# When the gate's sum is split and multiplied, in a hybrid convolution and RG-LRU layer

## The chip, the cores and the metric

The kernel runs on one core of a Trainium2 chip, in one launch. The metric is the time of one execution on the device in microseconds (us), taken as the median of several runs. A profiled execution also leaves a trace, which records when each instruction ran on each engine: PE (TensorE, matrix products), PEld (its weight loads), DVE (VectorE), ACT (ScalarE), POOL (GpSimd) and SP (the queue that issues the DMAs).

## The reference, cut to what matters

One layer on 512 latent tokens and 256 context tokens of width 2048. The input projection has six column groups; the gate `gt_l`, which the change is about, scales the output projection.

```python
mod_lat = silu(c) @ w_ada + b_ada
sh_l, sc_l, gt_l = split(mod_lat, 3)
...
hl = rmsnorm(x, norm_g) * (1 + sc_l) + sh_l
b, c, u, g, v, q = split(hl @ w_in)
ya = b * conv3(c * u) * silu(g)
xb = conv4(v) + bias            # also of the context tokens
yb = (scan_forward(xb) + scan_backward(xb)) * silu(q)
out = rmsnorm(x + gt_l * (concat(ya, yb) @ w_out), final_g)
```

Each scan is an RG-LRU: two block-diagonal products of `xb` give the gates r and i, from r come the decay a and the factor sqrt(1-a^2), and h = a h + b runs along the tokens.

## The kernel before, in words

**Products.** Every 32-bit operand is split into a rounded high part and the rest (`whi`, `wlo`; `xhi`, `hlo`), and a product is three matmuls, high by high, low by high and high by low (L83 to L85, `mm3`). The high part of a weight piece is made by ACT (L73), the low part by DVE (L74).

**Steps.** The main loop has 78 steps. A step takes one weight piece of 128 by 1024, which is half of a 128-wide column tile: 8 blocks of three matmuls on PE. Columns come in the order of `BC_TILES`: after a few first tiles the eight `v` tiles, then from step 22 (`S_C0`) on b, g, c, u, b, g and so on, two steps each. In step s the program issues the load of piece s+3, the split of piece s+2, the first four blocks of piece s on PE, what the table `mid` holds for step s, the other four blocks, the evacuation of the column tile that the step before finished, and last what the table `bg` holds for s. All engines run their own instructions strictly in this order; nothing reorders them later.

**The recurrence.** From step 22 on one of eight RG-LRU groups is worked off every seven steps. For group m with b = 22 + 7m: `l_prep` at b splits its weights into `lwh` and `lwl` (ACT L448, DVE L449) and its input into two tiles `xs` (ACT L454, DVE L455); `l_gate`, at the middle of steps b+2 to b+5, puts four matmuls (L468 to L471) into the two-bank tile `plru`, which ACT reads twice (L474, L475); `l_exp` at b+5 runs tanh and exp on ACT (L483, L485); `l_mul` at b+6 squares on POOL into `lx` (L490) and multiplies on DVE (L491), once for each direction; `l_sqrt` and `l_scan` come at b+7 and b+8. `lx` has one buffer, so the second square waits for the first multiplication.

**The gate's sum.** In steps 6 to 22 DVE adds up `wgt` weighted by silu(c) into `gacc` (L518, `gt_acc`), partition by partition. What is left is the sum over the 128 partitions, in four parts of 512 columns: `gt_split` casts a part into a high and a low tile (ACT L526, DVE L527), and `gt_sum` multiplies both by a matrix of ones (two matmuls, L534) and copies the result back into `gacc` (L537, for the last part L539). Its first reader is the output projection, near step 78. Before the change, part j is split at the end of step 28 + 7j, the step in whose end `l_mul` stands too, and its products stand in the middle of step 29 + 7j. The split's tiles are `lwh` and `lwl`, one buffer each, which `l_prep` uses as well.

Of the kernel before, what the change touches and what calls it, by code (L numbers as in the profile page):

```python
# [8 lines left out]
F32R = mybir.dt.float32r  # L9
# [40 lines left out]
def tile_hybrid_layer(ctx, tc, xt, ct, xn, wada, wgt, bgt, wa_, wbc, wout, lruw, par, ident, fg, out):  # L50
# [186 lines left out]
    for k in range(KT):  # L237
# [7 lines left out]
        j = k % 4  # L245
# [129 lines left out]
    lp = [None]  # L375
# [144 lines left out]
    gsp = {}  # L520

    def gt_split(j):
        hi = lp[0].tile([128, 512], F32R, name="lwh")
        lo = lp[0].tile([128, 512], F32R, name="lwl")
        g = gacc[:, 512 * j:512 * j + 512]
        nc.scalar.copy(hi, g)  # L526
        nc.vector.tensor_tensor(lo, g, hi.bitcast(F32), op=ALU.subtract)  # L527
        gsp[j] = hi, lo
# [13 lines left out]
    S_C0 = 2 * (N_FIRST + NM)  # L542
    bg, mid = {}, {}

    def at(step, f, *args, q=bg):
        q.setdefault(step, []).append((f, args))


    for m in range(NM):
        b = S_C0 + 7 * m  # L550
# [17 lines left out]
        at(S_V + i // 2, gt_load, i)  # L568
        at(S_V + 1 + i // 2, gt_acc, i)
    for j in range(4):  # L570
        at(S_C0 + 7 * j + 6, gt_split, j)
        at(S_C0 + 7 * j + 7, gt_sum, j, q=mid)
    at(1, lambda: nc.sync.dma_start(gacc[0:1, :], bgt))
    at(2, ctx_stat)
    at(3, ctx_stat2)
# [38 lines left out]
    for s in range(N_BC):  # L614
# [14 lines left out]
        hi, lo = wsp.pop(s)  # L629
# [83 lines left out]
    for q in range(N_D):  # L713
# [16 lines left out]
        hi, lo = wsp.pop(s)  # L730
# [98 lines left out]
```

## Time and profile before

| | |
|---|---|
| median of 3 runs | 832.32 us (829.97, 832.32, 1050.14) |
| profiled execution, its own time | 829.7 us |
| its span, first to last instruction | 827.8 us |
| PE busy | 793.9 us, 96% of the span |
| DVE, ACT, POOL busy | 478.6, 366.6, 89.7 us |
| granted clock of TensorE, mean | 0.99 |

The profiled execution is 1.9 us longer than its span; that part lies around the first and the last instruction. PE is the engine to look at: what it does not spend on matmuls is 34 us, and the question is where these lie. A busy time of PE does not say at which clock it worked; the granted clock of a stretch does.

### The profile page before, as it was taken

The numbers are of one execution on the slowest core, as the hardware profiler recorded it, in microseconds if no ns is written. First come the engines' busy times: TensorE is split into PE (matmuls) and PEld (weight loads), VectorE is DVE, ScalarE is ACT, GpSimd is POOL, SyncE is SP. The second block draws the span as 40 slices with busy tenths as digits, with TensorE's granted clock in tenths as the row PEclk, the third lists the DMA queues.
The fourth block names the chain that finished last, engine by engine and source line by source line (L and its number), as shares of the span: only waits on it lengthen the run. The fifth ranks groups of instructions, "written<-read, shape, count | busy, mean of one in ns | idle before, by whom it ended". The sixth has DMA issues, their size and how long they took to land. (4 is left out here: it accounts for less than half of the span.)

```text
span 827.8 us, 13520 instructions
## 1 busy us (share of the span) xinstructions
PE 793.9 (96%) x5712; PEld 682.4 (82%) x5712; DVE 478.6 (58%) x643; ACT 366.6 (44%) x458; POOL 89.7 (11%) x64
## 2 busy tenths in 40 slices
PE   6899899999999999898979999999999999999995
PEld 2787787889999998787868888888888888888884
DVE  3644345897886884463737273747385844344665
ACT  4312225441111125757566676665767533232234
POOL 0000003400000000202020302120212002020210
PEclk9999999999999999999999999999999999999999
DMA  9999987326556545232313223333232752323205
GB/s 341 417 416 411 349 313 236 103 77 224 183 182 235 194 166 168 73 115 76 115 51 111 72 72 106 116 97 116 76 109 94 287 181 92 112 92 109 95 1 203
DMA packets 36494, 136.31 MB, mean 165 GB/s; under 512 B 4049, under 2 KB 6353, under 8 KB 31697
## 3 DMA queue, kind: packets, MB, share of 16 engines
q1 hardware_dynamic: 36434, 135.45, 46.4%
q8 instruction: 45, 0.74, 0.4%
q14 instruction: 15, 0.12, 0.0%
HBM read 131.24 MB, written 4.19 MB: 164 GB/s over the span
## 5 line engine op out<-in xcount | busy, mean ns | idle before, releaser
L84 PE MATMUL bacc<-xhi,wlo 128*128 128x512 f32 x736 | 282.6, 384 | 2.2 <-issue 1.6
L83 PE MATMUL bacc<-xhi,whi 128*128 128x512 f32 x736 | 283.2, 385 | 0.8 <-ACT xhi L202 0.4
L85 PE MATMUL bacc<-hlo,whi 128*128 128x512 f32 x736 | 281.7, 383 | 2.3 <-issue 2.1
L74 DVE TENSOR_TENSOR wlo<-raw,whi 128x1024 fp32r<-128x1024 f32 (+1 forms) x129 | 157.5, 1225 | 212.0 <-ACT whi L73 210.7
L73 ACT CAST whi<-raw 128x1024 fp32r<-128x1024 f32 (+1 forms) x129 | 132.6, 1031 | 219.7 <-PE bacc L85 130.8
L84 PEld LDWEIGHTS bacc<-xhi,wlo 128*128 128x128 f32 x736 | 140.5, 191 | 25.7 <-DVE wlo L74 5.2
L85 PEld LDWEIGHTS bacc<-hlo,whi 128*128 128x128 f32 x736 | 140.4, 191 | 22.9 <-issue 2.5
L83 PEld LDWEIGHTS bacc<-xhi,whi 128*128 128x128 f32 x736 | 140.5, 191 | 22.5 <-ACT whi L73 0.7
L739 PE MATMUL bacc<-whi,yhi 128*128 128x512 f32 x224 | 85.1, 380 | 0.5 <-DVE dg L669 0.5
L740 PE MATMUL bacc<-wlo,yhi 128*128 128x512 f32 x224 | 84.9, 379 | 0.0
L741 PE MATMUL bacc<-whi,ylo 128*128 128x512 f32 x224 | 84.9, 379 | 0.0
L478 POOL TENSOR_TENSOR li<-li,xb 128x768 f32<-128x768 f32 x16 | 30.8, 1923 | 384.1 <-ACT li L475 384.1
L474 ACT ACTIVATE lr<-plru,pt 64x768 f32<-64x768 f32 x32 | 28.7, 895 | 54.3 <-PE plru L471 54.3
L267 ACT ACTIVATE xhi<-xhi,sh 128x512 fp32r<-128x512 f32 x15 | 10.8, 722 | 85.9 <-DVE xhi L266 85.9
L739 PEld LDWEIGHTS bacc<-whi,yhi 128*128 128x128 f32 x224 | 42.3, 189 | 7.1 <-DVE dg L669 1.1
L741 PEld LDWEIGHTS bacc<-whi,ylo 128*128 128x128 f32 x224 | 42.3, 189 | 6.0
L740 PEld LDWEIGHTS bacc<-wlo,yhi 128*128 128x128 f32 x224 | 42.3, 189 | 5.9
L518 DVE SCALAR_TENSOR_TENSOR gacc<-raw,cs,gacc 128x1024 f32<-128x1024 f32 x32 | 39.6, 1279 | 0.0
L84 PE MATMUL bacc<-xchi,wlo 128*128 128x256 f32 x128 | 35.2, 275 | 0.0
L85 PE MATMUL bacc<-hclo,whi 128*128 128x256 f32 x128 | 35.2, 275 | 0.0
L83 PE MATMUL bacc<-xchi,whi 128*128 128x256 f32 x128 | 35.2, 275 | 0.0
L223 PEld LDWEIGHTS bacc<-rada,cs 128*32 128x32 f32 x2048 | 29.5, 110 | 5.9 <-issue 5.5
(168 smaller groups left out, 875.4 us busy)
## 6 DMA issues: line engine op xcount, KB each, us to landing
raw<-in_wbc SPq DMA_DIRECT2D x82, 512.0 KB, 3.6
rada<-in_wada SPq DMA_DIRECT2D x32, 1024.0 KB, 10.4
raw<-in_wgt SPq DMA_DIRECT2D x32, 512.0 KB, 4.6
raw<-in_wout SPq DMA_DIRECT2D x32, 512.0 KB, 3.5
raw<-in_wa_ SPq DMA_DIRECT2D x16, 448.0 KB, 11.4
xhi<-in_xt SPq DMA_DIRECT2D x16, 256.0 KB, 4.6
xr<-in_xn SPq DMA_DIRECT2D x4, 1024.0 KB, 7.8
xchi<-in_ct SPq DMA_DIRECT2D x16, 128.0 KB, 4.4
```

The source lines that it names most:

```text
L73: nc.scalar.copy(hi[:, :n], raw[:, :n])
L74: nc.vector.tensor_tensor(lo[:, :n], raw[:, :n], hi[:, :n].bitcast(F32), op=ALU.subtract)
L83: nc.tensor.matmul(acc, wh, hh, start=first, stop=False)
L84: nc.tensor.matmul(acc, wl, hh, start=False, stop=False)
L85: nc.tensor.matmul(acc, wh, hl, start=False, stop=last)
L223: nc.tensor.matmul(o[32 * q:32 * q + 32], cs[:, 8 * p + j, :], r[:, j, q, :], start=p + j == 0, stop=p + j == 8, skip_group_check=True)
L474: nc.scalar.activation(lru["r", d][o], pf[0:64, :TA], AF.Sigmoid, bias=b[0:64])
L478: nc.gpsimd.tensor_tensor(lru["i", d], lru["i", d], xb[m], op=ALU.mult)
L518: nc.vector.scalar_tensor_tensor(gacc[:, s], gtq.pop(i), cs[:, k, 0:1], gacc[:, s], op0=ALU.mult, op1=ALU.add)
L739: nc.tensor.matmul(accs[t], yh[:, ts], wh, start=kk == 0, stop=False)
L740: nc.tensor.matmul(accs[t], yh[:, ts], wl, start=False, stop=False)
L741: nc.tensor.matmul(accs[t], yl[:, ts], wh, start=False, stop=kk == KT - 1)
```

## The change

`gt_split` takes the tiles `ctile` and `cutile`, one buffer each, in which the evacuations of the c and u columns keep their values (L390, L394), instead of `lwh` and `lwl`. The four splits stand at the end of steps 23, 25, 31 and 33 instead of 28, 35, 42 and 49, and their products at the middle of steps 25, 27, 33 and 35 instead of 29, 36, 43 and 50. Nothing is computed in another way. In the changed kernel the lines of these functions are one higher (L527, L528, L535, L538, L540).

```diff
     def gt_split(j):
-        hi = lp[0].tile([128, 512], F32R, name="lwh")
-        lo = lp[0].tile([128, 512], F32R, name="lwl")
+
+        hi = lp[0].tile([128, 512], F32R, name="ctile")
+        lo = lp[0].tile([128, 512], F32R, name="cutile")
         g = gacc[:, 512 * j:512 * j + 512]
         nc.scalar.copy(hi, g)
         nc.vector.tensor_tensor(lo, g, hi.bitcast(F32), op=ALU.subtract)
...
     for j in range(4):
-        at(S_C0 + 7 * j + 6, gt_split, j)
-        at(S_C0 + 7 * j + 7, gt_sum, j, q=mid)
+        b = S_C0 + 1 + 2 * j + 4 * (j // 2)
+        at(b, gt_split, j)
+        at(b + 2, gt_sum, j, q=mid)
```

On DVE, at the end of step 28 and in step 29, the kernel before has this (`lt` and `lx` are tiles of `l_mul`; the two L74 rows make the low parts of the weight pieces for steps 30 and 31):

```order
L74 TENSOR_TENSOR wlo<-raw,whi 128x1024 x2
L491 SCALAR_TENSOR_TENSOR lt<-lx,lt 128x768 x2
L527 TENSOR_TENSOR lwl<-gacc,lwh 128x512
L74 TENSOR_TENSOR wlo<-raw,whi 128x1024
L449 TENSOR_TENSOR lwl<-lwr,lwh 128x512
```

and the changed kernel this:

```order
L74 TENSOR_TENSOR wlo<-raw,whi 128x1024 x2
L491 SCALAR_TENSOR_TENSOR lt<-lx,lt 128x768 x2
L74 TENSOR_TENSOR wlo<-raw,whi 128x1024
L449 TENSOR_TENSOR lwl<-lwr,lwh 128x512
```

The low part of the gate's sum no longer stands behind the two multiplications of `l_mul`.

On ACT, in steps 22 to 25, the kernel before has this (L448 and L454 are `l_prep` of group 0, L474 and L475 read the first `l_gate`):

```order
L454 CAST xs_3419<-xb 64x768
L73 CAST whi<-raw 128x1024 x2
L474 ACT_TABLE_LOAD
L474 ACTIVATE lr<-plru,pt 64x768
L475 ACTIVATE li<-plru,pt 64x768
L73 CAST whi<-raw 128x1024
```

and the changed kernel this:

```order
L454 CAST xs_3419<-xb 64x768
L73 CAST whi<-raw 128x1024
L527 CAST ctile<-gacc 128x512
L73 CAST whi<-raw 128x1024
L474 ACT_TABLE_LOAD
L474 ACTIVATE lr<-plru,pt 64x768
L475 ACTIVATE li<-plru,pt 64x768
L73 CAST whi<-raw 128x1024
```

The first cast of the gate's sum now stands ahead of a weight piece, of a table load and of the two readers of `plru`, and reads what the last `gt_acc` of step 22 writes.

## Rows read from the trace of the kernel before

**Rows 1.** The page: the span, and PE's busy time.

```profile
span 827.8 us, 13520 instructions
PE 793.9 (96%) x5712; PEld 682.4 (82%) x5712; DVE 478.6 (58%) x643; ACT 366.6 (44%) x458; POOL 89.7 (11%) x64
```

**Rows 2.** Waits of PE, 200 to 500 us: engine, line, releaser: total, times, longest.

```profile
PE bacc L534 <- DVE lwl L527: 12.5, 4, 4.5
```

**Rows 3.** Timeline around the third part, ACT, then DVE: start, length, instruction.

```profile
426.90 0.61 ACT L526 CAST lwh<-gacc 128x512 fp32r<-128x512 f32 x1
...
428.37 0.95 DVE L491 SCALAR_TENSOR_TENSOR lt<-lx,lt 128x768 f32<-128x768 f32 x1
430.97 0.96 DVE L491 SCALAR_TENSOR_TENSOR lt<-lx,lt 128x768 f32<-128x768 f32 x1 [1.65 <-POOL lx L490]
431.84 0.69 DVE L527 TENSOR_TENSOR lwl<-gacc,lwh 128x512 fp32r<-128x512 f32 x1
```

**Rows 4.** Timeline of PE: two matmuls one step apart, then the four sums.

```profile
335.17 0.38 PE L84 MATMUL bacc<-xhi,wlo 128*128 128x512 f32 x1
...
340.35 0.38 PE L84 MATMUL bacc<-xhi,wlo 128*128 128x512 f32 x1
...
340.78 0.39 PE L534 MATMUL bacc<-lwh,onesr 128*128 128x512 f32 x1
...
343.97 0.38 PE L83 MATMUL bacc<-xhi,whi 128*128 128x512 f32 x1
...
383.05 0.39 PE L534 MATMUL bacc<-lwh,onesr 128*128 128x512 f32 x1
...
386.86 0.38 PE L83 MATMUL bacc<-xhi,whi 128*128 128x512 f32 x1
...
427.64 0.43 PE L534 MATMUL bacc<-lwh,onesr 128*128 128x512 f32 x1
...
433.17 0.63 PE L83 MATMUL bacc<-xhi,whi 128*128 128x512 f32 x1
...
474.86 0.39 PE L534 MATMUL bacc<-lwh,onesr 128*128 128x512 f32 x1
...
478.04 0.38 PE L83 MATMUL bacc<-xhi,whi 128*128 128x512 f32 x1
```

**Rows 5.** Windows: stretch, length, busy PE, PEld, DVE, ACT, POOL, PE's clock, DMA share, GB/s.

```profile
387.10:390.70 3.60, 3.60 (x10) 2.86 (x9) 0.51 (x1) 3.58 (x5) 0.00 (x0) 0.53 0.47 146
...
433.20:438.40 5.20, 5.20 (x14) 4.11 (x13) 1.41 (x3) 4.95 (x7) 0.00 (x0) 0.50 0.32 101
...
500.00:696.00 196.00, 196.00 (x920) 171.60 (x919) 112.55 (x124) 121.64 (x138) 25.60 (x15) 1.00 0.37 128
```

**Rows 6.** Timeline of PE: the first matmuls of the gates in steps 31 and 34.

```profile
354.33 0.40 PE L468 MATMUL plru<-xs,lwh 128*128 128x512 f32 x1
...
372.00 0.40 PE L468 MATMUL plru<-xs,lwh 128*128 128x512 f32 x1
```

**Rows 7.** Timeline of steps 23 to 25: DVE, then ACT, then PE's gate in step 25.

```profile
309.27 2.48 DVE L518 SCALAR_TENSOR_TENSOR gacc<-raw,cs,gacc 128x1024 f32<-128x1024 f32 x2
...
309.67 1.05 ACT L73 CAST whi<-raw 128x1024 fp32r<-128x1024 f32 x1 [4.13 <-PE bacc L85]
310.74 1.28 ACT L474 ACT_TABLE_LOAD   x1
312.96 0.90 ACT L474 ACTIVATE lr<-plru,pt 64x768 f32<-64x768 f32 x1 [0.94 <-PE plru L471]
...
317.93 0.40 PE L468 MATMUL plru<-xs,lwh 128*128 128x512 f32 x1
```

**Rows 8.** Timeline of ACT and DVE: square root, preparation and scan after the third sum.

```profile
435.30 1.58 ACT L495 ACTIVATE lt<-lt 128x768 f32<-128x768 f32 x2
...
437.29 1.69 ACT L454 CAST xs<-xb 64x768 fp32r<-64x768 f32 x2
...
438.15 1.94 DVE L455 TENSOR_TENSOR xs<-xb,xs 64x768 fp32r<-64x768 f32 x2
```

## The prediction, made before the changed kernel was run

> **What bounds the kernel now.** The page comes first: PE is busy for 793.9 of 827.8 us [rows 1], so a change can gain only where PE is not, or where it works at a lower clock. The waits of PE say where: between 200 and 500 us PE waits for one thing alone, four times, 12.5 us in all, the low part of the gate's sum [rows 2]. The timeline shows why, at the third of the four: ACT had cast the high part by 427.5, but DVE works in order, and ahead of the low part stand the two multiplications of l_mul, the second of which waits for POOL's square until 430.97, so that the low part is made only from 431.84 on [rows 3]. PE, which had done the high part's product at 427.64, goes on with the columns at 433.17 [rows 4]. Nobody needs this sum before the output projection; PE waits for it only because its products stand there in its order.
>
> **What the four places cost.** A step without a gate is 5.18 us (335.17 to 340.35 [rows 4]), which is 24 matmuls at 0.216. Without waiting, the two products of a sum would take 0.43. From the first product to the next column matmul it is 3.19, 3.81, 5.53 and 3.18 us [rows 4], so 2.76, 3.38, 5.10 and 2.75 are lost, 14.0 in all.
>
> That is not everything. Behind the second and the third wait the granted clock is 0.53 and 0.50, the lower of the two levels (1.2 against 2.4 GHz), for 3.6 and 5.2 us, and PE's order is full there [rows 5]. The engine had stood idle just before; behind the two shorter waits there is no such stretch. At half the clock half of the time is lost, so about 0.47 x 3.6 = 1.7 and 0.5 x 5.2 = 2.6 us.
>
> A second way to the same sum needs no clock: from one sum's first product to the next lie seven steps, four of them with a gate. Three steps with a gate take 17.67 us (354.33 to 372.00 [rows 6]), one 5.89. So 4 x 5.89 + 3 x 5.18 + 0.43 = 39.53 would do. It is 42.27, 44.59 and 47.22 [rows 4]: 2.74, 5.06 and 7.69 lost, and 2.75 behind the last sum. That makes 18.2 us, as do 14.0 and 4.3. I take 18.2.
>
> The Trainium skill ("TensorE: Matmul & The Clock Gate", section "Seeing it yourself") warns that clock records on trn2 have been seen to be unreliable. If they were so here, the 4.3 us would not exist and the gain would be 14.0. The way without the clock speaks against that: the time is missing between matmuls that have nothing to wait for.
>
> **What the change removes.** It takes the low part out of DVE's order behind l_mul and the products out of the steps that follow l_mul. All four waits go with it if the new places have none.
>
> **What it adds, and whether it is covered.** Each step that gets a sum has two more matmuls and each step that loses one has two fewer: nothing. The casts and subtractions are as many as before (0.61 on ACT, 0.69 on DVE [rows 3]). No DMA moves, so neither SP's queue nor POOL's is passed by anything.
>
> Step 23: the cast reads what the last gt_acc writes, and this ends at 309.27 + 2.48 = 311.75 [rows 7]. ACT, which would have begun the next weight piece at 309.67, stands still until then. Behind the cast are queued that piece (1.05), the table load (1.28) and the two readers of plru (0.90 each): 311.75 + 0.61 + 1.05 + 1.28 + 1.80 = 316.5. PE waits for them only at the next gate, 317.93 [rows 7], so 1.4 us are left. The low part is done about 1 us after the cast, near 313.5, and its product comes behind the gate of step 25, at 318.7. The weight piece that is late by 2.7 us is for step 26, from 321 on.
>
> Steps 25, 31 and 33: the split stands behind the readers of the gate of its own step, and its product two steps, some 11 us, later. The work between on DVE is longest in steps 30 and 31 (evacuation of a u column and the scans, 9 us); the low part follows it and one weight piece, and I reckon it 4 us ahead of its product in step 33. The tiles ctile and cutile are free: the columns c and u use them at steps 28, 30, 36 and 38, after the products of steps 27 and 35 have read them.
>
> **What is late next.** When PE no longer waits, it comes to the next gate earlier by what it waited, while the chain to that gate is still l_mul's: the second multiplication, its square root (0.79), the cast of the weights (0.61), the two casts of xs (1.69), and the last subtraction (0.97) [rows 3, 8]. That is 4.06 us behind the multiplication's end. After the third sum it ends at 431.93 + 4.06 = 436.0. PE would be at this gate two steps after 427.64, that is 48 matmuls or 10.36 us later, at 438.0. So 2.0 us are left. By the same sums, with their own multiplications, I get 4.0, 3.5 and 3.0 us after the first, second and fourth. In front of step 33, where DVE runs the evacuation of u and the scans ahead of a weight piece's low part, 1.9 us are left. These margins are thin beside what is removed, but each is positive, so I cost the new places at nothing. The ends are 0 and, if a chain is 4 to 5 us longer than I reckon, waits of about 1, 1, 2.5 and 1.5, or 6 us.
>
> From 500 to 696 us PE is busy without a gap at full clock while four more groups of the recurrence pass [rows 5], so an earlier start there is kept to the end.
>
> **The sum.** 829.7 is the profiled execution's time. 829.7 - 18.2 = 811.5. The two runs that lie together are 829.97 and 832.32, so 0.3 and 2.6 above it, and the median is the upper one. I forecast 812.5.
>
> **Rivals.** *A part comes back.* The chains above are late by some us, or gt_acc ends later than in this trace (each us beyond 1.4 is a us of PE in step 25). Such waits would be shorter than the two that lowered the clock. 1 to 6 us come back: 813 to 819. For it: margins of 1.4 to 2.0 us, worked out from one execution. Against it: the durations in the rows hardly vary.
>
> *The clock's part stays.* If the low clock has another cause than the idle time before it, only 14.0 go: 815.7. Against it: 196 us without a gap show none of it.
>
> *The sum moves nothing.* If the new products waited for something that I do not see (a buffer, gt_acc), about as long as the old ones did, the time stays at 830 to 832. Against it: ctile's and cutile's readers are steps away.
>
> *Slower: the wait moves to the gates, and grows.* The place is the first gate of the next group, steps 31, 38, 45 and 52. Its chain runs over ACT, POOL and DVE in turn, and I have put it 2.0 to 4.0 us ahead of PE. It would have to be as far behind PE as the low part was, 2.8 to 5.1 us, to cost what was gained, so some 7 us later than I work out; that is the point from which it decides. At 10 us, each wait is 3 us longer than the old one and the clock falls behind all four: 12 and some 4 us, near 846. Against it: after the fourth sum nothing like that is seen in any later group, where no sum stands in the way.
>
> **How the numbers follow.** The forecast has 0.76 (811 to 814.5), a part coming back 0.15, the clock's part staying 0.04, nothing moved 0.03, slower 0.02. For 8 times in 10 with the spread of runs of 2.4 us I take 809.5 to 819, which holds the second case and the third. Two per cent, about what a measurement of this kernel can tell from no change, are 16.6 us: 815.7 against the median. The forecast lies 1.5 to 4 us below that. Beside the lower run, 829.97, the bound would be 813.4, and a part of the forecast would be above it. So faster by over 2% gets 0.72, within 2% 0.26, slower 0.02.
>
> **What would show it.** In the profile after, PE's waits between 200 and 500 us should have no row for the sum, the clock should be 1.00 from 300 to 500 us, and the sums should follow their neighbours at 0.22 us. ACT's first cast of the sum should end about 0.6 us behind the last gt_acc, with the readers of plru done before the gate in step 25. A wait of PE on plru, on xs or on a weight piece near steps 25, 31, 33 or 45 would show a margin wrong; a wait for the sum in a new place would show the whole forecast wrong.

## The result, and the profile after

| | before | after |
|---|---|---|
| median | 832.08 us (829.97, 831.83, 832.32, 1050.14) | 811.54 us (810.92, 811.36, 811.72, 813.70) |
| profiled execution | 829.7 us | 810.92 us |
| first gate to last gate, see below | 311.79 us | 293.59 us |

The run of 1050.14 us lies far outside the others and is not counted in the ratio, which is 0.9769, with a 95% interval of 0.9745 to 0.9793: 2.3% faster. The forecast was 812.5 for the median and 811.5 for the profiled execution.

The page after has the span and PE's busy time, to be read beside [rows 1]:

```profile
span 809.1 us, 13525 instructions
PE 786.8 (97%) x5712; PEld 678.2 (84%) x5712; DVE 480.4 (59%) x643; ACT 366.8 (45%) x458; POOL 89.7 (11%) x64
```

PE works off as many matmuls as before and is busy for 7.1 us less, since matmuls at the lower clock count as longer. Of this, 1.4 us lie ahead of the first gate, where the profile before has a stretch at the lower clock, near 39 us, that the change does not touch. The other 11.6 us by which the span is shorter were idle time of PE.

The waits of PE over the whole execution after (total, times, longest), which answer to [rows 2]:

```profile
PE plru L246 <- ACT sq L242: 4.2, 2, 4.0
PE bacc L85 <- issue: 2.5, 1, 2.5
PE plru L246 <- DVE sq L240: 1.8, 2, 1.6
...
PE bacc L741 <- DVE dg L671: 0.5, 1, 0.5
```

There is no row for the gate's sum any more. What is left lies at the start and in the output projection, and the kernel before had it too. The timeline of PE after, at the first sum, answers to [rows 4]:

```profile
318.01 0.28 PE L471 MATMUL plru<-xs,lwl 128*128 128x256 f32 x1
318.12 0.40 PE L535 MATMUL bacc<-ctile,onesr 128*128 128x512 f32 x1
318.36 0.39 PE L535 MATMUL bacc<-cutile,onesr 128*128 128x512 f32 x1
318.59 0.38 PE L83 MATMUL bacc<-xhi,whi 128*128 128x512 f32 x1
```

From the sum's first product to the next column matmul it is 0.47 us, where the third sum took 5.53 before. The windows after show the clock of the middle (columns as in [rows 5]):

```profile
380.00:427.00 47.00, 47.00 (x223) 41.13 (x222) 27.46 (x31) 32.99 (x37) 8.06 (x5) 1.00 0.30 97
427.00:480.00 53.00, 53.00 (x252) 46.39 (x251) 35.92 (x36) 37.77 (x41) 8.38 (x5) 1.00 0.36 116
480.00:684.00 204.00, 204.00 (x957) 178.60 (x956) 118.49 (x131) 124.73 (x146) 29.90 (x19) 1.00 0.36 125
```

From 380 to 684 us PE has no gap and the clock is 1.00.

**A measure without the start.** What PE does ahead of the first gate, in step 24, is the same in all kernels here, but took from 311.5 to 314.1 us in the executions that were profiled. So I compare the stretch from the first gate's first matmul (L468) to the last gate's last (L471). Its two ends in the timeline of PE before, then after:

```profile
312.06 0.40 PE L468 MATMUL plru<-xs,lwh 128*128 128x512 f32 x1
...
623.85 0.28 PE L471 MATMUL plru<-xs,lwl 128*128 128x256 f32 x1
```

```profile
311.54 0.40 PE L468 MATMUL plru<-xs,lwh 128*128 128x512 f32 x1
...
605.13 0.28 PE L471 MATMUL plru<-xs,lwl 128*128 128x256 f32 x1
```

623.85 - 312.06 = 311.79 and 605.13 - 311.54 = 293.59: 18.20 us less. What is left of the 18.7 by which the span is shorter, 0.5, is the start.

### The profile page after: what moved, and what is told of

It reads as the page before. It is cut to its first block, busy times and chain, and to the rows that moved or that the text cites. A ratio compares the mean times of both kernels' runs of the same rounds, so it can differ in the third digit from the quotient of the medians.

```text
span 809.1 us, 13525 instructions
## 1 busy us (share of the span) xinstructions
PE 786.8 (97%) x5712; PEld 678.2 (84%) x5712; DVE 480.4 (59%) x643; ACT 366.8 (45%) x458; POOL 89.7 (11%) x64
## 4 chain that ended last, share of the span: by engine, by line
PE 95%; DMA 1%; DVE 1%; issue 1%; ACT 1%; SPq 0%; ACTq 0%
PE bacc L83 22%; PE bacc L84 22%; PE bacc L85 21%; PE bacc L741 6%; PE bacc L742 6%; PE bacc L743 6%; PE bacc L223 4%; DMA xhi<-in_xt 1%; PE plru L470 1%; PE plru L468 1%; PE plru L85 1%; PE plru L742 1%; PE plru L741 1%; PE plru L84 1%; PE plru L83 1%; PE plru L743 1%
## 5 line engine op out<-in xcount | busy, mean ns | idle before, releaser
L74 DVE TENSOR_TENSOR wlo<-raw,whi 128x1024 fp32r<-128x1024 f32 (+1 forms) x129 | 157.6, 1225 | 198.9 <-ACT whi L73 197.6
L478 POOL TENSOR_TENSOR li<-li,xb 128x768 f32<-128x768 f32 x16 | 30.8, 1925 | 365.3 <-ACT li L475 365.3
L474 ACT ACTIVATE lr<-plru,pt 64x768 f32<-64x768 f32 x32 | 28.7, 895 | 53.2 <-PE plru L471 53.0
```

What stands on the lines that cost most here:

```text
L74: nc.vector.tensor_tensor(lo[:, :n], raw[:, :n], hi[:, :n].bitcast(F32), op=ALU.subtract)
L474: nc.scalar.activation(lru["r", d][o], pf[0:64, :TA], AF.Sigmoid, bias=b[0:64])
L478: nc.gpsimd.tensor_tensor(lru["i", d], lru["i", d], xb[m], op=ALU.mult)
```

## The experiments

My theory was the prediction's: PE lost 14.0 us in four waits for the low part, because that stood behind l_mul on DVE, and some 4 us more at the lower clock behind them; in the new places the sum costs its eight matmuls and nothing else. The rivals were that the lead of one and a half steps or the steps 23 to 35 themselves make the gain, that the low clock has another cause, and that PE is not as near to the next chain as I reckoned. The table has all runs; "gates" is the stretch just named, from the profiled execution.

| run | median, us | first gate at | gates | beside the changed kernel | expected |
|---|---|---|---|---|---|
| e1, split ahead of l_mul | 813.76 | 311.50 | 294.96 | +1.37 | +1.3 |
| e2, half a step of lead | 818.91 | 313.22 | 299.94 | +6.35 | +3.4 to 5.1 |
| e3, only parts 1 and 2 moved | 820.39 | 312.32 | 302.57 | +8.98 | +5.4 |
| e4, only parts 0 and 3 moved | 824.71 | 313.47 | 306.00 | +12.41 | +12.7 |
| e5, chain longer by 2 additions | 812.85 | 312.14 | 293.59 | 0.00 | 0 |
| e6, by 6 | 815.46 | 314.06 | 295.40 | +1.81 | +2.0 |
| e7, by 10 | 819.82 | 311.79 | 300.72 | +7.13 | +7.2 |
| e8, no sum at all | 810.49 | 312.37 | 291.75 | -1.84 | -1.8 |
| e9, the kernel before again | 833.36, one run | 313.15 | 314.40 | +20.81 | +18.2, or 16 to 22 |
| e10, the same | 833.06, one run | 312.62 | 314.58 | +20.99 | +18.2, or 16 to 22 |
| e11, the changed kernel again | 813.36, one run | 313.91 | 293.59 | 0.00 | 0 |

### e1: the order on DVE alone

In the kernel before, the splits are put into the tables ahead of the recurrence's groups:

```diff
+    for j in range(4):
+        at(S_C0 + 7 * j + 6, gt_split, j)
     for m in range(NM):
...
     for j in range(4):
-        at(S_C0 + 7 * j + 6, gt_split, j)
         at(S_C0 + 7 * j + 7, gt_sum, j, q=mid)
```

> The kernel before, with one thing changed: the split of each part of the gate's sum stands ahead of l_mul in the end of the same step (28, 35, 42, 49), not behind it. Tiles lwh and lwl and the products' places (29, 36, 43, 50) stay. Theory (PE waited because the low part stood behind l_mul's two multiplications on DVE): the low part is made at once when its cast is done, near 340.1, 383.0, 429.1 and 474.1 on the clock of the trace before, against products at 341.0, 383.3, 427.9 and 475.1. Only the third part is late, by about 1.3 us (its DVE order begins with a gate's evacuation), and an idle time as short as that lowers no clock. So 829.7 - 18.2 + 1.3 = 812.8 us for the profiled execution, 813 to 815 for the median. Rival (the lead of one and a half steps, or the steps 23 to 35 themselves, make the gain; a lead of half a step leaves PE waiting wherever it stands): 825 to 832 us, four waits of PE for the low part left.

Measured: 813.76 us, ratio 0.9776 (0.9745 to 0.9808). The waits of PE between 200 and 690 us:

```profile
PE bacc L534 <- DVE lwl L527: 1.0, 1, 1.0
```

One wait is left, at the third sum, as expected: there the evacuation of a column, which waits for ACT, stands ahead of the split. The gates take 1.37 us more than in the changed kernel. Since `l_mul` has no work on ACT and the split none on POOL, it is DVE's order alone that was changed, and the tiles, the steps and the longer lead together add 1.37 of the 18.20 us. Half a step of lead is enough where nothing that waits for another engine stands ahead. The rival falls.

### e2: half a step of lead in the new place

```diff
-        at(b, gt_split, j)
+        at(b + 1, gt_split, j)
```

> The changed kernel with the splits one step later (24, 26, 32, 34) and the products where the change has them (25, 27, 33, 35), so the lead is half a step as it was before. Theory (what counts is what stands ahead of the split on DVE and ACT): the first three parts are ready 2 us or more ahead of their products and cost nothing. The fourth now stands behind l_exp on ACT (step 34), whose second exponential ends near 377.8 on the clock of the changed kernel's trace; its cast ends near 378.4, its low part near 379.1, and PE is at its products from 375.5 on: 3.4 us lost, and if the idle time lowers the clock, as one of 3.08 us did before, 1 to 2 us more. 811.5 + 3.4 to 5.1 = 815 to 816.6 us. Rival (a lead of one and a half steps is needed anywhere): four waits of 2 to 3 us, 820 us or more. Rival (lead plays no part and any place in these steps will do): 811.5 us.

Measured: 818.91 us, ratio 0.9845 (0.9814 to 0.9875). PE waits for one part alone, the fourth. Timeline of ACT, then of PE, then the window behind:

```profile
377.77 1.76 ACT L485 ACTIVATE lr<-lr,nsp 128x768 f32<-128x768 f32 x2
379.44 0.60 ACT L527 CAST ctile<-gacc 128x512 fp32r<-128x512 f32 x1
...
376.99 0.38 PE L85 MATMUL bacc<-hlo,whi 128*128 128x512 f32 x1
380.09 0.80 PE L535 MATMUL bacc<-ctile,onesr 128*128 128x512 f32 x1 [2.72 <-ACT ctile L527]
380.92 0.79 PE L535 MATMUL bacc<-cutile,onesr 128*128 128x512 f32 x1
381.51 0.63 PE L83 MATMUL bacc<-xhi,whi 128*128 128x512 f32 x1
...
380.10:386.20 6.10, 6.07 (x13) 4.43 (x14) 3.81 (x4) 1.97 (x2) 1.68 (x2) 0.50 0.27 87
```

The cast stands behind the two exponentials, as expected, and three parts cost nothing. The fourth cost 6.35 and not 5.1 at most, because the clock was at the lower level for 6.1 us behind an idle time of 2.72. I had expected 1 to 2 us for it. So the lead does matter in this place: not by its length, but by what stands inside it.

### e3 and e4: two parts at a time

```diff
-        at(b, gt_split, j)
-        at(b + 2, gt_sum, j, q=mid)
+        if j in (1, 2):                     # e4: (0, 3)
+            at(b, gt_split, j)
+            at(b + 2, gt_sum, j, q=mid)
+        else:
+            at(S_C0 + 7 * j + 6, gt_split, j)
+            at(S_C0 + 7 * j + 7, gt_sum, j, q=mid)
```

with `ctile` and `cutile` for the moved parts and `lwh` and `lwl` for the others.

> Only the second and the third part (j = 1 and 2) take the change's places and tiles; the first and the fourth stay in steps 28/29 and 49/50 with lwh and lwl. Theory (each place is worth what it cost alone: wait and low clock): gained are 3.38 + 1.7 and 5.10 + 2.6, so 829.7 - 12.8 = 816.9 us for the profiled execution, with two waits of about 2.5 us left and a clock of 1.00 behind both. Rival (the low clock has another cause than the idle time ahead of it): the clock still falls somewhere between 380 and 440 us, and 829.7 - 8.5 = 821.2 us.

> Only the first and the fourth part (j = 0 and 3) take the change's places and tiles; the second and the third stay in steps 35/36 and 42/43. Theory: gained are 2.76 + 2.75, so 829.7 - 5.5 = 824.2 us for the profiled execution, with two waits of about 3.1 and 4.5 us left and the granted clock near 0.5 for 3 to 5 us behind each. Rival (the low clock has another cause, such as the waits adding up over all four places): no low clock, and about 820 us.

Measured: 820.39 us for e3 (ratio 0.9865, 0.9826 to 0.9903) and 824.71 for e4 (0.9912, 0.9881 to 0.9942). The waits of PE, 200 to 690 us, in e3 and in e4:

```profile
PE bacc L536 <- DVE lwl L529: 5.0, 2, 2.6
```

```profile
PE bacc L536 <- DVE lwl L529: 7.1, 2, 4.5
```

The waits stand where the first profile of before had them and are nearly as long: 2.59 and 2.46 us in e3 (2.45 both there), 2.61 and 4.52 in e4 (3.08 and 4.51). e4 is as expected. e3 is not: it is 3.6 us slower. The windows of e3 behind its two waits:

```profile
345.40:348.60 3.20, 3.20 (x9) 2.49 (x8) 0.16 (x1) 3.18 (x5) 0.00 (x0) 0.50 0.54 164
468.20:471.40 3.20, 3.20 (x9) 2.49 (x9) 0.78 (x2) 3.17 (x4) 0.00 (x0) 0.50 0.47 164
```

Behind the first and the fourth wait, which had left the clock alone in the first profile, it now fell to the lower level for 3.2 us each, and a little more at the edges. Half of that, 1.6 us each, is what was missing. So the idle time does cost clock, but my reading that the two shorter waits do not was the reading of one execution.

### e5, e6 and e7: how near PE is to the next chain

In the changed kernel, needless additions of 128 by 512 on DVE ahead of l_mul of group 2 make the chain to the gate in step 45 longer; 2, 6 or 10 of them:

```diff
     def l_mul(m):
+        if m == 2:
+            t = lp[0].tile([128, 512], F32, name="cutile")
+            for _ in range(10):
+                nc.vector.tensor_tensor(t, gacc[:, :512], gacc[:, 512:1024], op=ALU.add)
```

> The changed kernel with two needless additions of 128x512 on DVE (into cutile, which nobody reads then) ahead of l_mul of group 2 in step 42; a pair of such instructions takes 0.72 us each in the trace, so the chain to the gate in step 45 is 1.2 to 1.4 us longer. Theory (PE is 2.0 us behind this chain: the last xs is done at 428.6, the gate stands at 430.6 in the trace of the changed kernel): no wait of PE, 811.5 us. Rival (the margin isn't there, PE waits already for what the chain makes): 812.8 us.

> The same with six additions, 3.7 to 4.3 us. Theory: DVE is late with the low part of the piece for step 45 (done at 425.7, wanted at 428.0, so 2.3 us are left) and with xs (2.0 left); PE waits 1.7 to 2.3 us in all, the clock stays at 1.00 because the idle time is shorter than the 2.45 us that left it alone in the kernel before. 811.5 + 2.0 = 813.5 us. Rival (the margin is larger than it looks, since PE isn't bound to this chain): 811.5 us. Rival (any idle time lowers the clock): 815 us or more.

> The same with ten additions, 6.1 to 7.2 us. Theory: PE waits 4.1 to 5.2 us in step 45, most of it for the low part of a weight piece, and the granted clock is near 0.5 for about 5 us behind it, though no sum of the gate is near: 811.5 + 4.7 + 2.5 = 818.7 us. It is the slower rival of the prediction, at one place. Rival (the low clock belonged to the gate's sum or to steps 36 and 43, not to idle time): 816.2 us, clock at 1.00.

Measured: 812.85, 815.46 and 819.82 us (ratios 0.9773, 0.9748 to 0.9798; 0.98, 0.978 to 0.982; 0.985, 0.9827 to 0.9873); the gates take 0.00, 1.81 and 7.13 us more than in the changed kernel. In e5 PE waits for nothing between 200 and 690 us. In e6 it waits once (timeline of PE):

```profile
432.47 0.48 PE L84 MATMUL bacc<-xhi,wlo 128*128 128x512 f32 x1 [1.56 <-DVE wlo L74]
```

The timeline of e7, DVE, then PE, and the window behind:

```profile
421.23 7.22 DVE L491 TENSOR_TENSOR cutile<-gacc 128x512 f32<-128x512 f32 x10
428.37 0.95 DVE L495 SCALAR_TENSOR_TENSOR lt<-lx,lt 128x768 f32<-128x768 f32 x1
...
431.84 1.22 DVE L74 TENSOR_TENSOR wlo<-raw,whi 128x1024 fp32r<-128x1024 f32 x1
...
428.26 0.38 PE L83 MATMUL bacc<-xhi,whi 128*128 128x512 f32 x1
433.11 0.79 PE L84 MATMUL bacc<-xhi,wlo 128*128 128x512 f32 x1 [4.47 <-DVE wlo L74]
...
433.20:437.50 4.30, 4.30 (x10) 3.43 (x11) 4.06 (x5) 4.14 (x6) 0.00 (x0) 0.50 0.39 122
```

The additions take 7.22 us, PE waits 4.47 of them, for the low part of a weight piece, and the clock falls behind it with no sum of the gate near. Two additions cost nothing, six cost 1.81 of their 4.3 us. So there is a margin at this place, of about 2.5 us, and beyond it each us of DVE is one of PE, with the clock's loss on top in e7. It is the weight piece that decides, not xs, as the prediction had put it; see below. This is the prediction's slower rival at one place: it is real, and the changed kernel stays 2.5 us short of it there. The median of e6 is 2 us above its expectation. In its profiled execution, 815.47, the first gate came at 314.06, 2.5 us later than in the changed kernel's profile and ahead of the added instructions; its other three runs were not profiled.

### e8: no sum

The four calls of `gt_split` and of `gt_sum` are left out.

> The changed kernel without the four splits, the eight products and the four copies: the gate's sum over the partitions is left out. Theory (in the new places the sum costs PE its eight matmuls and nothing else): 8 x 0.22 = 1.8 us less, 809.7 us. Rival (the sum in its new places still delays something, through ACT's order in steps 23 to 27 or the banks of the accumulators): 3 us or more less, below 808.5 us.

Measured: 810.49 us, ratio 0.9741 (0.9719 to 0.9763); the gates take 1.84 us less, 8 matmuls at 0.23. In its new places the sum costs PE its products and nothing else. Nothing more is to be had from moving it.

### e9, e10 and e11: the same kernels again

> The kernel before, unchanged, profiled once more. Open is whether the low clock behind a wait goes by the wait's length (then again behind the second and the third sum alone, 4.3 us) or differs from one execution to the next (it fell behind waits of 2.46 to 2.61 us when only some parts were moved, but not behind the 2.45 us of the first profile). If by length: from the first gate to the last 311.8 us, as in the first profile. If by the execution: 310 to 315.5 us, with low clock behind any of the four.

> As the run before it: the same kernel, one more profile. By length: 311.8 us from the first gate to the last, low clock behind the second and the third sum alone. By the execution: another set of low stretches, 310 to 315.5 us.

> The changed kernel, unchanged, profiled once more. Without waits there is nothing for the clock to fall behind from the first gate to the last, so this stretch should take 293.6 us again, to 0.1 us, whatever the time ahead of it does.

Measured: 314.40 and 314.58 us from gate to gate for the kernel before, against 311.79 in the first profile; 293.59 for the changed kernel, to the digit the same. The windows behind the first and the fourth wait, in e9, then in the first profile of before:

```profile
344.70:348.00 3.30, 3.28 (x8) 2.64 (x9) 1.10 (x1) 2.43 (x3) 0.00 (x0) 0.51 0.23 77
...
479.70:484.00 4.30, 4.28 (x13) 3.51 (x14) 1.81 (x3) 3.71 (x4) 0.00 (x0) 0.66 0.36 122
```

```profile
344.00:348.00 4.00, 4.00 (x20) 3.52 (x19) 0.71 (x1) 3.81 (x5) 0.00 (x0) 1.00 0.39 131
478.00:482.30 4.30, 4.30 (x21) 3.75 (x20) 1.79 (x3) 4.03 (x4) 0.00 (x0) 1.00 0.33 122
```

In e9 and e10 the clock fell behind all four waits, in the first profile behind two. The waits are of one length in all three (2.45 to 2.46, 3.07 to 3.08, 4.51 to 4.52 and 2.45 to 2.46 us). So the waits belong to the kernel and the low clock to the execution. The change removes 18.2 us in one execution and 20.8 to 21.0 in others.

## Why the prediction was right

**What bounds the kernel.** Right. The four waits for the low part were PE's only ones in the middle, and they came from l_mul on DVE: e1 takes l_mul from ahead of the split and changes nothing else, and gets all but 1.37 of 18.20 us.

**What the four places cost.** The sum was 18.2 for the profiled execution, and the stretch from gate to gate became shorter by 18.20. The part of it that the low clock made was mis-sized for other executions: 4.3 in the first profile, but some 7 in e9 and e10 (20.8 and 21.0 less 14.0 of waiting). The step behind it was the sentence that there is no low clock behind the two shorter waits; e3, e9 and e10 show that there can be. The median of before may hold such executions too, which would fit a gap of 20.5 us between the medians, more than the 18.2 of one profile. No clock is recorded for its runs, so this stays an inference, but the mean granted clock of other runs of the same kernel speaks for it: it is 0.990 in the first profile, 0.984 and 0.986 in e9 and e10, and from 0.984 to 0.992 in the seven runs beside e1 to e4, which were made on one chip. My forecast for the median, 812.5, came out 1.0 us too high. It stood 1.0 above the one for the profiled execution, and the median was 0.6 above it; the profiled execution itself came out 0.6 below its forecast of 811.5, and 0.5 of that is the start, which I had not forecast.

The Trainium skill's warning ("TensorE: Matmul & The Clock Gate", section "Seeing it yourself") that clock records on trn2 have been seen to be unreliable did not hold for the stretches shown here: at a granted clock of 0.50 matmuls follow each other at 0.43 us (ten in the 4.30 us of e7) and not at 0.216.

**What the change adds.** Nothing, as forecast: e8 finds its eight matmuls and no more. One step of the working was wrong, on the safe side. I let the first cast wait for the last gt_acc of step 22. The timeline after, DVE, then ACT:

```profile
308.74 2.48 DVE L518 SCALAR_TENSOR_TENSOR gacc<-raw,cs,gacc 128x1024 f32<-128x1024 f32 x2
...
310.12 0.62 ACT L527 CAST ctile<-gacc 128x512 fp32r<-128x512 f32 x1 [4.93 <-DVE gacc L518]
310.64 1.04 ACT L73 CAST whi<-raw 128x1024 fp32r<-128x1024 f32 x1
311.70 1.28 ACT L474 ACT_TABLE_LOAD   x1
312.99 0.90 ACT L474 ACTIVATE lr<-plru,pt 64x768 f32<-64x768 f32 x1
313.90 0.90 ACT L475 ACTIVATE li<-plru,pt 64x768 f32<-64x768 f32 x1
```

The two accumulations run from 308.74 to 311.22, and the cast begins at 310.12, half way: the first of them writes the half of `gacc` that part 0 is in. So plru was read by 314.80, and the next gate stands at 317.41 (0.71 ahead of the sum at 318.12): 2.6 us of margin, where I had 1.4.

**What is late next.** The sums were right, but at the gate in step 45 it is another instruction that PE would wait for first. The timeline after ahead of this gate, DVE, then PE (compare [rows 3, 8]):

```profile
423.56 0.96 DVE L491 SCALAR_TENSOR_TENSOR lt<-lx,lt 128x768 f32<-128x768 f32 x1 [1.65 <-POOL lx L490]
424.44 1.22 DVE L74 TENSOR_TENSOR wlo<-raw,whi 128x1024 fp32r<-128x1024 f32 x1
...
426.67 1.94 DVE L455 TENSOR_TENSOR xs<-xb,xs 64x768 fp32r<-64x768 f32 x2
...
428.22 0.38 PE L84 MATMUL bacc<-xhi,wlo 128*128 128x512 f32 x1
...
430.59 0.40 PE L468 MATMUL plru<-xs,lwh 128*128 128x512 f32 x1
```

From the multiplication's end at 424.52 to the last xs at 428.61 it is 4.09 us (4.06 forecast), and 1.98 are left to the gate (2.0). The other three came out at 3.9, 3.9 and 3.1 (4.0, 3.5 and 3.0). But the gate in step 45 takes only the first of the two xs, which is done about 0.97 earlier; the second is for the gate in step 46. So xs has some 3 us. Nearer is the low part of the piece for step 45, which stands behind the same multiplication on DVE: it is done at 425.66 and wanted at 428.22, 2.56 us. e6 agrees: 4.3 us of additions less 2.56 is 1.8, and 1.81 was measured; and in e7 it is this piece that PE waits for.

A smaller margin lies ahead of step 33, and there the prediction had both the instruction and the size (1.9 us). The timeline after, DVE, then PE:

```profile
357.73 1.22 DVE L74 TENSOR_TENSOR wlo<-raw,whi 128x1024 fp32r<-128x1024 f32 x1
...
360.93 0.38 PE L84 MATMUL bacc<-xhi,wlo 128*128 128x512 f32 x1
```

The low part of the piece for step 33 is done at 358.95 and wanted at 360.93, so 1.98 us are left. No run made this chain longer.

**The rivals.** None happened. For a part to come back, a chain had to be longer by 2.0 us ahead of step 33 or by 2.6 ahead of the gates in steps 25 and 45; e6 made the last. The slower one needed some 7 us more at each gate; e7 made 7.2 at one of them and lost 7.13 us there, against the 7.69 that the third sum had cost.

## What to carry to other kernels

When the engine that sets the time waits for a small by-product, look at what stands ahead of its maker in that engine's order before giving it more lead: one place ahead of a chain that waits for another engine was worth 17 of 18 us here, and the same half step of lead behind a pair of exponentials cost 6 of them again. Work out what is late next as a margin in us, at each place, from the rows of the chain; then a result without a wait is not luck. And take the gain of a removed wait from more than one execution if the clock may fall behind it.

## What I had not expected of the hardware

A wait of one length lowers TensorE's clock in some executions and not in others: 2.45 us of idle time was followed by the clock at 1.00 in the first profile of before, and 2.45 or 2.46 by the lower level (0.50 to 0.51, for some 3 us) at the last sum of e3 and at the first of e9. PE at the first sum of before, in its first profile, then at the last sum of e3 (the windows behind them are above):

```profile
343.63 0.50 PE L534 MATMUL bacc<-lwl,onesr 128*128 128x512 f32 x1 [2.45 <-DVE lwl L527]
...
467.05 0.50 PE L536 MATMUL bacc<-lwl,onesr 128*128 128x512 f32 x1 [2.46 <-DVE lwl L529]
```

The waits of 1.0 us in e1 and 1.6 in e6 were followed by no such stretch; each wait of 2.59 us or more in the middle was followed by one. The length alone does not decide: in the start, between 36 and 39.1 us, an idle time of 2.12 us was followed by the lower level in the first profile of before, and one of 2.46 ahead of the same matmul by none in the changed kernel's. What decides stays open.

In the new place one subtraction took longer. The timeline after, POOL, then DVE:

```profile
320.20 1.83 POOL L478 TENSOR_TENSOR li<-li,xb 128x768 f32<-128x768 f32 x1 [166.54 <-ACT li L475]
...
321.40 1.18 DVE L528 TENSOR_TENSOR cutile<-gacc,ctile 128x512 fp32r<-128x512 f32 x1 [4.03 <-ACT ctile L527]
```

L528 took 0.68 or 0.69 in the other three parts and 1.18 here, where POOL's multiplication runs until 322.03; it ends 0.55 behind that. The Trainium skill ("SBUF — State Buffer", section "SBUF: two separate sides") says that a DVE instruction with two SBUF inputs and a GpSimd one that reads SBUF exclude each other for a whole instruction. This row agrees, and no run here tests it by itself. A second pair in the trace looks alike: L410 at 373.74 took 1.07 us, where it took 0.69 at 327.86 and at 420.35, and ends 0.54 behind POOL's L478, which ran from 372.44 to 374.27. At L528 it costs nothing, since the product stands 8 us later.
